# The order of the recurrence's strided views, and the row length of accumulating DMA transfers

## The chip, the cores and the metric

The kernel runs on one core of a Trainium2 chip. The metric is device time in microseconds (us) of one execution, as the median of several runs. The engines are named as in the profile: PE is TensorE (matmuls; PEld is its weight load), DVE is VectorE, ACT is ScalarE, POOL is GpSimd and SP is SyncE, which issues the loads. 16 DMA engines serve the core.

## The reference

One decoder block on 256 tokens of width 1024, in float32. An input projection gives the operands of two token mixers: a gated linear recurrence with 8 heads of 128 (HGRN2), and causal attention with 8 heads of 128, which at this length is one block. Each mixer's output is projected, the two are merged by sigmoid gates, projected again, added to the residual and normalised. A SwiGLU network with 2816 hidden channels and a second normalisation follow. The change touches the recurrence:

```python
step(state, (qc, kc, vc, lfc)):        # one chunk of 64 tokens
    G = cumsum(lfc)
    decay = exp(G[t] - G[s])  for s <= t, else 0
    scores = einsum('decay[t,s,d] qc[t,d] kc[s,d] -> scores[t,s]')
    o = scores @ vc + (qc * exp(G)) @ state
```

The result does not depend on the chunk length, so that a kernel may cut the 256 tokens in any other way.

## The kernel before, in words

**Tokens.** The 256 tokens lie in two halves of 128. The second half is mirrored (ORDER), so that the two halves count their tokens towards each other. Features are on the partitions, and the free dimension of the recurrence's tiles is (half u, head h, token t), 2 x 8 x 128 = 2048 floats; one half of a tile is 4 KB.

**The recurrence by levels** (hgrn_steps). Instead of 64-token chunks, the kernel doubles: at level l, runs of n = 2^l tokens are paired with the next run of n tokens, for l from 0 to 6, and the scores of each pair are made by one matmul per head. Qt holds the queries times the decay so far, Kt the keys times theirs, tot the decay products of the runs, SD the scores. In each level, half of the tokens are "later" and the other half "earlier"; through the mirroring the later run of a pair in half 0 lies where the earlier run lies in half 1. The two functions `earlier` and `later` (lines 414 to 418) give a view of exactly those 1024 elements of a tile:

```python
[[P, nh], [2 * n, 64 // n], [H * P + n, NT], [1, n]]     # heads, blocks, half, tokens of a run
```

Each level then has four steps. ScalarE copies the earlier elements of Kt into KL (line 444). TensorE multiplies, head by head, KL as weights with the later elements of Qt (line 449), 8 matmuls of 128 columns in plain float32, each of which the profile shows as two records. VectorE writes those scores that belong to the same block into SD, with a predicated copy per four heads, whose mask is a constant from shape_constants (line 451). VectorE multiplies the later elements of Qt and the earlier ones of Kt by the neighbour's decay (lines 458 and 459), and makes tot of the next level (line 462).

**Other work of that time.** These steps stand among the products of the input projection, with which TensorE goes on between them. side.step() in the program interleaves the two. Outside of stretches in manual_schedule, a scheduler sets the order of the instructions on each engine from its own estimates.

**Weights.** Each weight tile of 1 MB comes in by a load on SP's queue (line 223, 128 rows of 8 KB, three buffers), ScalarE rounds it to the high part wh (line 224), VectorE subtracts to get the low part wl (line 226), and TensorE uses both in three products. A load can start when VectorE has read the buffer's previous content; the high and low parts have four buffers each.

**Weight sums.** For some products (gate hg, values mv, down projection) a scheme with 7 instead of 8 block products is used, which needs sums of weight blocks. The sums are made by DMA alone, from DRAM to DRAM (sum_weights, line 235): four plain copies and four accumulating transfers for each of four groups, 16 accumulating transfers of 1 MB in all. They are issued on POOL's queue one after the other, in the order of SUMS, each behind a tiny instruction on POOL that waits for a certain weight tile (SUMS_WITH). An accumulating transfer waits for the transfers that made its operands, and the weight load of a sum (raw<-u) waits for the last of them. The row length of the accumulating ones is set by max_dma_last_dim, 2048 bytes.

Of the kernel before, what the change touches and what calls it, by code (L numbers as in the profile page):

```python
# [14 lines left out]
ALU = mybir.AluOpType  # L15
# [40 lines left out]
def shape_constants():  # L56
    c = np.zeros((P, C_END), np.float32)
    i = np.arange(P)
    c[:, C_CAUSAL:C_CAUSAL + P] = np.where(i[None, :] <= i[:, None], 0.0, NEG)
    c[:, C_CAUSAL + 2 * P:C_MASK] = np.where(i[None, :] >= i[:, None], 0.0, NEG)  # L60
    half = P // 2
    inv = np.float32(10000.0) ** (-np.arange(half, dtype=np.float32) / np.float32(half))
    ang = np.arange(T, dtype=np.float32)[:, None] * inv.astype(np.float32)[None, :]
    cos = np.cos(ang.astype(np.float64)).astype(np.float32)[ORDER].T
    sin = np.sin(ang.astype(np.float64)).astype(np.float32)[ORDER].T
    c[:, C_COS:C_COS + T] = np.concatenate([cos, cos], 0)
    c[:, C_SIN:C_SIN + T] = np.concatenate([-sin, sin], 0)
    for l in range(LEVELS):
        n = 2 ** l
        b, r = i >> (l + 1), (i >> l) & 1  # L70
        m = (b[:, None, None, None] == np.arange(64 // n)[None, :, None, None]) & \
            (r[:, None, None, None] == np.arange(2)[None, None, :, None]) & np.ones((1, 1, 1, n), bool)
        c[:, C_MASK + l * P:C_MASK + (l + 1) * P] = m.reshape(P, P)
    return np.concatenate([np.eye(P, dtype=np.float32), c], 1)

# [68 lines left out]
def hybrid_layer_kernel(ctx: ExitStack, tc, x, xT, vecs, wts, ln1_w, ln1_b, ln2_w, ln2_b, consts, out):  # L144
# [90 lines left out]
    def sum_weights(behind):  # L235


        n = len(SUMS_WITH) - len(sums)
        dst, src, add = sums.pop(0)
        tick = ticks[:, n:n + 1]  # L240
        nc.vector.tensor_copy(tick, behind)  # L241
        tc.keep_in_program_order(nc.gpsimd.tensor_tensor(mark, tick, tick, op=ALU.add))  # L242
        more = dict(accum_op=ALU.add, max_dma_last_dim=2048) if add else {}
        tc.keep_in_program_order(nc.gpsimd.dma_start(source(dst), source(src), **more))  # L244

    def fetch(ahead=LOOKAHEAD):
# [162 lines left out]
    def free_view(ap, offset, dims):  # L409
        return bass.AP(ap.tensor, ap.offset + offset, [ap.ap[0]] + dims)  # L410
# [1 line left out]


    def earlier(z, n, h0=0, nh=H):
        return free_view(z, h0 * P, [[P, nh], [2 * n, 64 // n], [H * P + n, NT], [1, n]])

    def later(z, n, h0=0, nh=H):
        return free_view(z, h0 * P + n, [[P, nh], [2 * n, 64 // n], [H * P - n, NT], [1, n]])

    def hgrn_steps():  # L420
        Qt, SD = halves(slot("Qt")), halves(slot("SD"))
        nc.vector.tensor_mul(Qt, Qg, Fg)
        flat = lambda z: z.rearrange("p u h t -> p (u h t)")
        kq, kqh, kql = flat(Qg), slot("kqh", F32R), slot("kql", F32R)
        nc.vector.tensor_mul(kq, flat(Kt), kq)
        nc.scalar.copy(kqh, kq)
        nc.vector.tensor_sub(kql, kq, r32(kqh))
        for g in range(4):
            ps = aux.tile([P, 4, P], F32, tag="aux", name=f"sd{g}")
            cs = slice(g * 512, (g + 1) * 512)  # L430
            row = ps.rearrange("p h t -> p (h t)")
            nc.tensor.matmul(row, ones, kqh[:, cs], start=True, stop=False)
            nc.tensor.matmul(row, ones, kql[:, cs], start=False, stop=True)
            nc.vector.tensor_tensor(SD[:, g // 2, 4 * (g % 2):4 * (g % 2) + 4, :], ps,
                                    ident[:, None, :].to_broadcast([P, 4, P]), op=ALU.mult)
        yield
        Tt = slot("Tt")
        tot, size = Fg, NT * H * P
        off = 0
        for l in range(LEVELS):  # L440
            n = 2 ** l
            nb = 64 // n
            KL = klp.tile([P, H, P], F32, tag="kl", name=f"kl{l}")
            nc.scalar.copy(KL.rearrange("p h (b u i) -> p h b u i", u=NT, i=n), earlier(Kt, n))
            for g in range(2):
                ps = aux.tile([P, 4, P], F32, tag="aux", name=f"sc{l}_{g}")
                for a in range(4):
                    h = 4 * g + a
                    nc.tensor.matmul(ps[:, a, :], KL[:, h, :], later(Qt, n, h, 1), start=True, stop=True)  # L449
                m = masks[:, l, :].rearrange("p (b u i) -> p b u i", u=NT, i=n)  # L450
                nc.vector.copy_predicated(later(SD, n, 4 * g, 4),
                                          m[:, None, :, :, :].to_broadcast([P, 4, nb, NT, n]),
                                          ps.rearrange("p a (b u i) -> p a b u i", u=NT, i=n))

            first = free_view(tot, 0, [[2, H * nb], [size // NT + 1, NT], [0, n]])
            second = free_view(tot, 1, [[2, H * nb], [size // NT - 1, NT], [0, n]])
            flat = lambda z: z.rearrange("p h b u i -> p (h b) u i")
            nc.vector.tensor_mul(flat(later(Qt, n)), flat(later(Qt, n)), first)
            nc.vector.tensor_mul(flat(earlier(Kt, n)), flat(earlier(Kt, n)), second)
            if l < LEVELS - 1:  # L460
                nxt = Tt[:, off:off + size // 2]
                nc.vector.tensor_mul(nxt, free_view(tot, 0, [[2, size // 2]]), free_view(tot, 1, [[2, size // 2]]))
                off += size // 2
                tot, size = nxt, size // 2
            yield
        SL = klp.tile([P, H, P], F32, tag="kl", name="SL")
        for g in range(2):
            ps = aux.tile([P, 4, P], F32, tag="aux", name=f"sc7_{g}")
            for a in range(4):
                nc.tensor.matmul(ps[:, a, :], Kt[:, 0, 4 * g + a, :], Qt[:, 1, 4 * g + a, :], start=True, stop=True)  # L470
            nc.scalar.copy(SL[:, 4 * g:4 * g + 4, :], ps)
        yield
        yah[:] = [slot("yah", F32R).rearrange("p (h t) -> p h t", h=H)]
        yal[:] = [slot("yal", F32R).rearrange("p (h t) -> p h t", h=H)]
        for g in range(2):
            for u in range(NT):
                ps = aux.tile([P, 4, P], F32, tag="aux", name=f"o{g}{u}")
                for a in range(4):
                    h = 4 * g + a
                    hd = slice(h * P, (h + 1) * P)  # L480
                    if u == 1:
                        nc.tensor.matmul(ps[:, a, :], SL[:, h, :], hv[:, 0, hd], start=True, stop=False)
                    nc.tensor.matmul(ps[:, a, :], SD[:, u, h, :], hv[:, u, hd], start=(u == 0), stop=True)
                sq = hd2.tile([P, 4, P], F32, tag="sg", name=f"sq{g}{u}")
                st = sm.tile([P, 12], F32, tag="ost", name=f"ost{g}{u}")
                for a in range(4):
                    nc.scalar.activation(sq[:, a, :], ps[:, a, :], AF.Square, accum_out=st[:, a:a + 1])
                nc.vector.tensor_scalar(st[:, 4:8], st[:, 0:4], 1.0 / P, RMS_EPS, op0=ALU.mult, op1=ALU.add)
                nc.gpsimd.tensor_tensor(st[:, 8:12], st[:, 4:8], half, op=ALU.pow)
                row = hgs[:, u, g * 512:(g + 1) * 512].rearrange("p (a d) -> p a d", a=4)  # L490
                nc.vector.tensor_mul(row, row, ps)
                for a in range(4):
                    nc.scalar.mul(row[:, a, :], row[:, a, :], st[:, 8 + a:9 + a])
            yield
            for j in range(2):
                h0 = 4 * g + 2 * j
                pt = aux.tile([P, 2, T], F32, tag="aux", name=f"ot{g}{j}")
                for a in range(2):
                    for u in range(NT):
                        hd = slice((h0 + a) * P, (h0 + a + 1) * P)  # L500
                        nc.tensor.transpose(pt[:, a, u * P:(u + 1) * P], hgs[:, u, hd], ident)
                for a in range(2):
                    h = h0 + a
                    nc.scalar.activation(yah[0][:, h, :], pt[:, a, :], AF.Copy, scale=nw[:, h:h + 1])
                    nc.vector.scalar_tensor_tensor(yal[0][:, h, :], pt[:, a, :], nw[:, h:h + 1], r32(yah[0][:, h, :]),
                                                   op0=ALU.mult, op1=ALU.subtract)
        yield
# [487 lines left out]
```

## Time and profile before

| | us |
|---|---|
| median of 3 runs | 501.06 (501.01 to 501.81) |
| the profiled execution's own time | 501.59 |
| its span | 499.5 |
| PE busy | 488.8 |
| DVE busy | 380.5 |
| ACT busy | 299.3 |
| POOL busy | 92.4 |

The span is the time from the first to the last recorded instruction of one execution; the rest of the execution's own time lies around it. A group of instructions is named by line, engine and operation, and tiles by their names in the program, without buffer numbers. A time on the chain that ended last is time that the end depended on. A row of waits reads: the waiting engine and line, what released it, the total in us, how many times, and the longest. In the table by stretch, the DMA share is the mean busy share of the 16 engines, and can be a little over 1 where two transfers overlap on an engine.

### The profile page before, as it was taken

How to read it: one execution, taken by the hardware profiler on the slowest of the kernel's cores; microseconds unless marked ns; L12 is line 12 of the kernel's file. 1: busy time of each engine (PE TensorE's matmuls, PEld its weight loads, DVE VectorE, ACT ScalarE, POOL GpSimd, SP SyncE). 2: the span in 40 equal slices, each digit the busy share in tenths (PEclk: the TensorE clock that was granted, in tenths of full speed). 3: DMA queues.
4: the chain of work that ended last, by engine and by line, in shares of the span. 5: the costliest groups of instructions: out<-in, count | busy, mean ns of one | idle time of the engine just before them, and what ended most of it. 6: DMA issues, size and time to landing. Idle time of an engine off the chain costs nothing.

```text
span 499.5 us, 7868 instructions
## 1 busy us (share of the span) xinstructions
PE 488.8 (98%) x3176; PEld 447.8 (90%) x3176; DVE 380.5 (76%) x441; ACT 299.3 (60%) x396; POOL 92.4 (18%) x97
## 2 busy tenths in 40 slices
PE   8999999999999999999999999999999999999993
PEld 8999889999999999999999988888888888898883
DVE  4678889977788588689855789566687679688856
ACT  6698655427498779697553443354665666586610
POOL 0003370320000243377400000002212011000001
PEclk9999999999999999999999999999999999999997
DMA  7989999989998997649856555249999999999802
GB/s 241 363 298 365 368 309 319 248 322 308 349 337 261 308 339 244 241 166 411 295 226 228 193 207 211 88 168 357 290 312 320 343 312 306 300 337 371 289 1 85
DMA packets 26404, 137.83 MB, mean 276 GB/s; under 512 B 2560, under 2 KB 3712, under 8 KB 14592
## 3 DMA queue, kind: packets, MB, share of 16 engines
q1 hardware_dynamic: 16560, 100.63, 53.6%
q0 software_dynamic: 9808, 36.70, 28.3%
q8 instruction: 25, 0.41, 0.3%
q14 instruction: 11, 0.09, 0.1%
HBM read 136.27 MB, written 34.60 MB: 342 GB/s over the span
## 4 chain that ended last, share of the span: by engine, by line
PE 93%; DMA 3%; DVE 1%; SPq 1%; issue 0%; ACT 0%; DVEq 0%
PE fu L846 7%; PE fg L846 7%; PE fg L847 3%; PE fu L847 3%; DMA raw<-in_wts_dram 3%; PE sc L449 3%; PE wd L929 2%; PE wd L930 2%; PE wd L931 2%; PE mk L321 2%; PE zb L321 2%; PE zb L320 2%; PE zb L319 2%; PE hq L321 2%; PE hq L320 2%; PE hq L319 2%
## 5 line engine op out<-in xcount | busy, mean ns | idle before, releaser
L226 DVE TENSOR_TENSOR wl<-raw,wh 128x2048 fp32r<-128x2048 f32 (+2 forms) x100 | 214.6, 2149 | 76.9 <-ACT wh L224 76.6
L224 ACT CAST wh<-raw 128x2048 fp32r<-128x2048 f32 (+2 forms) x100 | 179.0, 1792 | 103.0 <-DMA raw<-in_wts_dram 26.5
L846 PE MATMUL fg<-x1p,wh 128*128 128x512 f32 x144 | 50.5, 394 | 0.0
L846 PE MATMUL fu<-x1p,wh 128*128 128x512 f32 x144 | 50.4, 394 | 0.0
L242 POOL TENSOR_TENSOR mark<-ticks 128x1 f32<-128x1 f32 x32 | 24.3, 760 | 135.6 <-DVE ticks L241 135.5
L847 PE MATMUL fg<-x1p,wl 128*128 128x256 f32 x144 | 40.0, 277 | 0.0
L847 PE MATMUL fu<-x1p,wl 128*128 128x256 f32 x144 | 39.9, 277 | 0.0
L846 PEld LDWEIGHTS fu<-x1p,wh 128*128 128x128 f32 x144 | 27.0, 187 | 6.2
L846 PEld LDWEIGHTS fg<-x1p,wh 128*128 128x128 f32 x144 | 27.0, 187 | 6.1
L847 PEld LDWEIGHTS fg<-x1p,wl 128*128 128x128 f32 x144 | 27.0, 188 | 0.1
L847 PEld LDWEIGHTS fu<-x1p,wl 128*128 128x128 f32 x144 | 27.0, 188 | 0.0
L244 POOL DMA_DIRECT2D u<-u x8 | 8.2, 1020 | 65.3 <-DMA u<-u 22.6
L319 PE MATMUL hf<-xTh,wh 128*128 128x256 f32 x64 | 19.1, 298 | 0.9 <-ACT wh L224 0.9
L321 PE MATMUL hf<-xTh,wl 128*128 128x256 f32 x64 | 19.0, 298 | 0.6 <-DVE wl L226 0.6
L244 POOL DMA_DIRECT2D u<-in_wts_dram x24 | 17.5, 732 | 10.0 <-DMA u<-in_wts_dram 8.5
L319 PE MATMUL za<-yah,wh 128*128 128x256 f32 x64 | 18.9, 295 | 0.0
L320 PE MATMUL hf<-xTl,wh 128*128 128x256 f32 x64 | 18.8, 294 | 0.0
L319 PE MATMUL mq<-xTh,wh 128*128 128x256 f32 x64 | 18.5, 289 | 0.0
L319 PE MATMUL mk<-xTh,wh 128*128 128x256 f32 x64 | 18.4, 287 | 0.0
L321 PE MATMUL mk<-xTh,wl 128*128 128x256 f32 x64 | 18.3, 286 | 0.0
L319 PE MATMUL gb<-xTh,wh 128*128 128x256 f32 x64 | 18.3, 286 | 0.0
L321 PE MATMUL ga<-xTh,wl 128*128 128x256 f32 x64 | 18.3, 285 | 0.0
(310 smaller groups left out, 1463.9 us busy)
## 6 DMA issues: line engine op xcount, KB each, us to landing
raw<-in_wts_dram SPq DMA_DIRECT2D x74, 1024.0 KB, 6.7
raw<-u SPq DMA_DIRECT2D x16, 1024.0 KB, 8.0
u<-in_wts_dram POOLq DMA_DIRECT2D x8, 1024.0 KB, 20.2
u<-u POOLq DMA_DIRECT2D x8, 1024.0 KB, 18.9
raw<-in_wts_dram SPq DMA_DIRECT2D x8, 256.0 KB, 4.8
xTr<-in_xT_dram SPq DMA_DIRECT2D x8, 128.0 KB, 4.8
raw<-in_wts_dram SPq DMA_DIRECT2D x2, 512.0 KB, 6.5
xr<-in_x_dram POOLq DMA_DIRECT2D x1, 1024.0 KB, 8.6
```

Of the source, the lines that this page charges most:

```text
L224: nc.scalar.copy(h[:, ks, :], raw[:, ks, :])
L226: eng.tensor_sub(l[:, ks, :], raw[:, ks, :], r32(h[:, ks, :]))
L242: tc.keep_in_program_order(nc.gpsimd.tensor_tensor(mark, tick, tick, op=ALU.add))
L244: tc.keep_in_program_order(nc.gpsimd.dma_start(source(dst), source(src), **more))
L319: nc.tensor.matmul(ps, wh[:, k, wcol], ah[:, kk, :], start=(kk == 0), stop=False)
L320: nc.tensor.matmul(ps, wh[:, k, wcol], al[:, kk, :], start=False, stop=False)
L321: nc.tensor.matmul(ps, wl[:, k, wcol], ah[:, kk, :], start=False, stop=(kk == KC - 1))
L449: nc.tensor.matmul(ps[:, a, :], KL[:, h, :], later(Qt, n, h, 1), start=True, stop=True)
L846: nc.tensor.matmul(ps, wh[:, k, wcol], x1p.both(k), start=(k == 0), stop=False)
L847: nc.tensor.matmul(ps[:, 0, :], wl[:, k, wcol], x1p[0, k, slice(0, T)], start=False, stop=(k == KC - 1))
L929: nc.tensor.matmul(ps, lh[:, k, :], wh[:, k, ns], start=n < 5 and i + k == 0, stop=False, **go)
L930: nc.tensor.matmul(ps, lh[:, k, :], wl[:, k, ns], start=False, stop=False, **go)
```

## The change

Three things change together, and the constants of the masks with them.

1. The views `earlier` and `later` go through the half first, then heads, blocks and the tokens of a run. They name the same elements in another order. The copy into KL, the moving operand of the score matmuls, the predicated copies and the columns of the masks follow that order.
2. The two products of a level on all 1024 elements become four, one per half, each on 512.
3. The accumulating transfers have rows of up to 8192 bytes.

```diff
@@ shape_constants
-        m = (b[:, None, None, None] == np.arange(64 // n)[None, :, None, None]) & \
-            (r[:, None, None, None] == np.arange(2)[None, None, :, None]) & np.ones((1, 1, 1, n), bool)
+        m = (b[:, None, None, None] == np.arange(64 // n)[None, None, :, None]) & \
+            (r[:, None, None, None] == np.arange(2)[None, :, None, None]) & np.ones((1, 1, 1, n), bool)
@@ sum_weights
-        more = dict(accum_op=ALU.add, max_dma_last_dim=2048) if add else {}
+        more = dict(accum_op=ALU.add, max_dma_last_dim=8192) if add else {}
@@
     def earlier(z, n, h0=0, nh=H):
-        return free_view(z, h0 * P, [[P, nh], [2 * n, 64 // n], [H * P + n, NT], [1, n]])
+        return free_view(z, h0 * P, [[H * P + n, NT], [P, nh], [2 * n, 64 // n], [1, n]])
 
     def later(z, n, h0=0, nh=H):
-        return free_view(z, h0 * P + n, [[P, nh], [2 * n, 64 // n], [H * P - n, NT], [1, n]])
+        return free_view(z, h0 * P + n, [[H * P - n, NT], [P, nh], [2 * n, 64 // n], [1, n]])
@@ hgrn_steps
-            nc.scalar.copy(KL.rearrange("p h (b u i) -> p h b u i", u=NT, i=n), earlier(Kt, n))
+            nc.scalar.copy(KL.rearrange("p h (b u i) -> p u h b i", u=NT, i=n), earlier(Kt, n))
...
-                m = masks[:, l, :].rearrange("p (b u i) -> p b u i", u=NT, i=n)
+                m = masks[:, l, :].rearrange("p (u b i) -> p u b i", u=NT, i=n)
                 nc.vector.copy_predicated(later(SD, n, 4 * g, 4),
-                                          m[:, None, :, :, :].to_broadcast([P, 4, nb, NT, n]),
-                                          ps.rearrange("p a (b u i) -> p a b u i", u=NT, i=n))
-
-            first = free_view(tot, 0, [[2, H * nb], [size // NT + 1, NT], [0, n]])
-            second = free_view(tot, 1, [[2, H * nb], [size // NT - 1, NT], [0, n]])
-            flat = lambda z: z.rearrange("p h b u i -> p (h b) u i")
-            nc.vector.tensor_mul(flat(later(Qt, n)), flat(later(Qt, n)), first)
-            nc.vector.tensor_mul(flat(earlier(Kt, n)), flat(earlier(Kt, n)), second)
+                                          m[:, :, None, :, :].to_broadcast([P, NT, 4, nb, n]),
+                                          ps.rearrange("p a (u b i) -> p u a b i", u=NT, i=n))
+
+            side = lambda z, off, u: free_view(z, off + u * H * P, [[2 * n, H * nb], [1, n]])
+            whole = lambda off: free_view(tot, off, [[2, H * nb], [0, n]])
+            for u in range(NT):
+                q, k = side(Qt, n - u * n, u), side(Kt, u * n, u)
+                nc.vector.tensor_mul(q, q, whole(u * (size // NT + 1)))
+                nc.vector.tensor_mul(k, k, whole(1 + u * (size // NT - 1)))
```

The order of the instructions on the engines stays nearly the same. On DVE, around the end of level 0 and the start of level 1 (sc_0_805 and sc_1_811 are the scores of level 0, wl the low part of a weight tile), there stands before:

```order
L451 COPY_PREDICATED SD<-cst,sc_0_805 128x256x2
L458 TENSOR_TENSOR Qt<-Qt,Fg 128x512x2
L241 COPY ticks<-wl_857 128x1
L462 TENSOR_TENSOR Tt<-Tt 128x128
L451 COPY_PREDICATED SD<-cst,sc_1_811 128x256x2
L226 TENSOR_TENSOR wl_895<-raw_893,wh_894 128x2048
L462 TENSOR_TENSOR Tt<-Tt 128x64
L459 TENSOR_TENSOR Kt<-Kt,Tt 128x256x2x2
```

And at the same place on DVE after the change:

```order
L451 COPY_PREDICATED SD<-cst,sc_0_805 128x2x256
L459 TENSOR_TENSOR Qt<-Qt,Fg 128x512 x2
L241 COPY ticks<-wl_859 128x1
L463 TENSOR_TENSOR Tt<-Tt 128x128
L451 COPY_PREDICATED SD<-cst,sc_1_811 128x2x256
L226 TENSOR_TENSOR wl_897<-raw_895,wh_896 128x2048
L463 TENSOR_TENSOR Tt<-Tt 128x64
L460 TENSOR_TENSOR Kt<-Kt,Tt 128x256x2 x2
```

Nothing has changed places; the products stand twice, and the views have the half ahead of the rest. Lines from 459 on have moved down by one.

On PE, where the score matmuls of level 0 stand among the gate product gb of the input projection, there stands before:

```order
L319 MATMUL gb_903<-xTh,wh_768 128x256
L449 MATMUL sc_0_805<-Qt,kl_803 128x128 x4
L449 MATMUL sc_1_811<-Qt,kl_803 128x128 x4
L320 MATMUL gb_903<-xTl,wh_768 128x256
L321 MATMUL gb_903<-xTh,wl_769 128x256
```

And at the same place on PE after the change:

```order
L319 MATMUL gb_905<-xTh,wh_768 128x256
L320 MATMUL gb_905<-xTl,wh_768 128x256
L449 MATMUL sc_0_805<-Qt,kl_803 128x128 x4
L449 MATMUL sc_1_811<-Qt,kl_803 128x128 x4
L321 MATMUL gb_905<-xTh,wl_769 128x256
```

The eight score matmuls of level 0 have moved behind one more matmul of gb. The matmuls of sd (line 433) move by one in the same way; the other rows of PE stand as they stood.

On POOL, the sums of the first group (u_3072: the gate hg) have before:

```order
L244 DMA u_3072_0_388<-in_wts_dram 512x512
L242 TENSOR_TENSOR mark<-ticks 128x1
L244 DMA u_3072_0_453<-in_wts_dram 512x512
L242 TENSOR_TENSOR mark<-ticks 128x1
L244 DMA u_3072_0_741<-in_wts_dram 16x16384
L242 TENSOR_TENSOR mark<-ticks 128x1
L244 DMA u_3072_0_516<-u_3072_0_388 512x512
```

And on POOL after the change:

```order
L244 DMA u_3072_0_388<-in_wts_dram 128x2048
L242 TENSOR_TENSOR mark<-ticks 128x1
L244 DMA u_3072_0_453<-in_wts_dram 128x2048
L242 TENSOR_TENSOR mark<-ticks 128x1
L244 DMA u_3072_0_741<-in_wts_dram 16x16384
L242 TENSOR_TENSOR mark<-ticks 128x1
L244 DMA u_3072_0_516<-u_3072_0_388 128x2048
```

The order is the same, and so are the plain copies (16 rows); the accumulating transfers have 128 rows of 2048 floats in place of 512 rows of 512.

## The prediction

> **What bounds the kernel now.** I read the page's first part, then what TensorE waited for, then a table by stretch, then the chain that ended last.
>
> ```profile
> span 499.5 us, 7868 instructions
> PE 488.8 (98%) x3176; PEld 447.8 (90%) x3176; DVE 380.5 (76%) x441; ACT 299.3 (60%) x396; POOL 92.4 (18%) x97
> ```
>
> What TensorE waited for, whole span (all of the answer):
>
> ```profile
> PE warm L366 <- DVE half L367: 1.1, 1, 1.1
> PE hf L319 <- ACT wh L224: 0.9, 1, 0.9
> PE hf L321 <- DVE wl L226: 0.6, 1, 0.6
> ```
>
> By stretch (TensorE, weight loads, VectorE, ScalarE, GpSimd busy, then granted clock, DMA share, GB/s):
>
> ```profile
> 27.00:76.00 49.00, 49.00 (x325) 45.27 (x324) 40.48 (x36) 36.28 (x39) 18.60 (x15) 1.00 0.97 338
> 76.00:91.00 15.00, 15.00 (x113) 14.65 (x112) 15.00 (x17) 7.48 (x7) 0.81 (x2) 1.00 0.81 233
> 91.00:160.00 69.00, 69.00 (x497) 65.09 (x497) 55.83 (x50) 43.52 (x43) 9.72 (x17) 1.00 1.00 316
> ...
> 330.00:427.00 97.00, 97.00 (x556) 84.66 (x555) 69.64 (x94) 58.47 (x80) 15.44 (x24) 1.00 1.00 310
> ```
>
> TensorE waits 2.6 us in all, every bit of it in the warm-up and the hf matmuls at the start, at full clock, and is busy for all of each stretch from 27 us on. So time is gained only by making matmuls shorter, and lost by anything that makes them wait. The second thing to see is the DMA share: 1.00 from 91 to 160 us and from 330 to 427 us, the two places where the accumulating transfers run. The transfer engines have nothing to spare there. Vector and Scalar time is not the bound: 55.8 and 43.5 of 69 us.
>
> **The score matmuls.** The changed views are read by TensorE only in the score matmuls of line 449. The chain gives one row per level, 16 records each (two per matmul):
>
> ```profile
> 78.48 2.67 PE sc L449 x16
> 86.77 1.92 PE sc L449 x16
> 99.85 1.79 PE sc L449 x16
> ```
>
> Level 0 takes 2.67/16 = 167 ns a record, level 1 120 ns, level 2 112 ns, and the later levels repeat 1.79. The levels differ only in the run length n of the view, 1, 2, 4 elements, after which it jumps to the other half of the tile, 4 KB away. After the change it stays in one half and skips n elements instead: level 0 reads every second element of one row of 128. I have no row of TensorE reading at that stride. Upper bound: it keeps 167 ns, since the runs are still one element long (gain 0, rival two). Lower bound: the contiguous rate, 112 ns, gain 16 x 55 = 0.88 us. Nearest row: level 1, which like the new level 0 uses two elements of each 16 bytes, 120 ns, gain 0.75 us. Level 1 itself can go from 120 to 112, gain 0 to 0.13 us. Together 0.75 to 1.01 us; I take 0.9, all of it on the path since TensorE waits for nothing here.
>
> [...]
>
> **The Vector and Scalar work.** From VectorE's timeline:
>
> ```profile
> 62.87 2.24 DVE L459 TENSOR_TENSOR Kt<-Kt,Fg 128x1024 f32<-128x1024 f32 x1
> ...
> 77.28 0.68 DVE L462 TENSOR_TENSOR Tt<-Tt 128x512 f32<-128x512 f32 x1
> ...
> 80.41 2.50 DVE L451 COPY_PREDICATED SD<-cst,sc 128x512 f32<-128x512 uint32 x1
> 82.50 2.50 DVE L458 TENSOR_TENSOR Qt<-Qt,Fg 128x1024 f32<-128x1024 f32 x1
> ...
> 89.69 1.23 DVE L459 TENSOR_TENSOR Kt<-Kt,Tt 128x1024 f32<-128x1024 f32 x1
> ...
> 90.98 1.33 DVE L451 COPY_PREDICATED SD<-cst,sc 128x512 f32<-128x512 uint32 x1
> ...
> 108.32 0.73 DVE L451 COPY_PREDICATED SD<-cst,sc 128x512 f32<-128x512 uint32 x1 [1.38 <-PE sc L449]
> ```
>
> The products: each product of 1024 elements becomes two of 512. The 512-element product at 77.28 reads both operands at a stride of two and takes 0.68, so a pair is 1.36. At level 0 that replaces 2.24 and 2.50: 2.0 us less. At levels 1 to 6 it replaces 1.23 or so, 12 times: 12 x 0.13 = 1.6 us more. The predicated copies of level 0 (2.50, twice) go to between 0.73 and 1.33 (level 1): 2.3 to 3.5 us less. The Scalar copy into kl at level 0 goes from its longest (1590 ns) to its median:
>
> ```profile
> L444 ACT COPY kl<-Kt x7: 1031/1051/1590, 32.5 to 141.0; 128x1024 f32<-128x1024 f32 x7
> ```
>
> Net, Vector is relieved of 2.7 to 3.9 us and Scalar of 0.5. Before 91 us this is hidden behind TensorE's own work; it buys slack and no time. The 0.13 us per product that come after 91 us delay the weight subtraction (L226) queued behind them on Vector; the nearest slack on Vector is 0.9 us (below; where a tile has only 0.06 us, Vector had idled 1.64 us before it), so they are covered too. TensorE's order changes at two points by one matmul, which costs nothing: the same instructions run back to back.
>
> **The accumulating transfers.** 16 of them, 1 MB each, go from 512 rows of 2 KB to 128 rows of 8 KB. TensorE does not wait for them, but the weight loads share the engines with them. Four stretches of the DMA queues: accumulates alone (95 to 99 us), both (159 to 165), weight loads alone (181 to 185), and 2 KB rows of the output (493 to 497):
>
> ```profile
> DMA packets 395, 0.87 MB, mean 217 GB/s; under 512 B 2, under 2 KB 2, under 8 KB 394
> ```
> ```profile
> q1 hardware_dynamic: 210, 1.59, 66.4%
> q0 software_dynamic: 212, 0.43, 38.9%
> ```
> ```profile
> DMA packets 207, 1.56 MB, mean 391 GB/s; under 512 B 16, under 2 KB 16, under 8 KB 16
> q1 hardware_dynamic: 207, 1.56, 94.5%
> ```
> ```profile
> DMA packets 239, 0.46 MB, mean 116 GB/s; under 512 B 16, under 2 KB 16, under 8 KB 238
> q1 hardware_dynamic: 238, 0.45, 30.2%
> ```
>
> On 16 engines, 4 us hold 64 engine-us. Alone, a 2 KB accumulated row takes 64/393 = 163 ns and an 8 KB weight row 64/191 = 335 ns. Side by side (q1 the loads, q0 the accumulates) they go row for row, 210 to 212. That is what the change turns round. An 8 KB accumulated row is not in the trace. Upper bound: four 2 KB rows, 652 ns. Lower bound: one plain 8 KB row, 335 ns. I take the upper one less what long rows save plain transfers: 2 KB rows occupy an engine for 0.302 x 64/222 = 87 ns, four of them 348, against 0.945 x 64/191 = 317 for one of 8 KB, 9% less. So about 595 ns.
>
> A weight load is 8 rows per engine. Beside an accumulate it now takes 8 x (335 + 163) = 4.0 us and will take 8 x (335 + 595) = 7.4 us, 3.4 us more (1.4 to 3.9 by the bounds). The accumulate itself takes 32 x 498 = 15.9 us now and 7.4 then, and its own work falls from 32 x 163 = 5.2 to 8 x 595 = 4.8 us. So loads are hit harder, but for half as long, and over an accumulate and its aftermath the loads lose nothing. What covers the 3.4 us is the distance between a weight tile's subtraction and the matmul that uses it. It varies. Vector:
>
> ```profile
> 103.45 2.30 DVE L226 TENSOR_TENSOR wl<-raw,wh 128x2048 fp32r<-128x2048 f32 x1
> ...
> 140.60 2.29 DVE L226 TENSOR_TENSOR wl<-raw,wh 128x2048 fp32r<-128x2048 f32 x1 [0.50 <-ACT wh L224]
> ...
> 170.30 2.29 DVE L226 TENSOR_TENSOR wl<-raw,wh 128x2048 fp32r<-128x2048 f32 x1 [1.64 <-ACT wh L224]
> ```
>
> and the matmuls that first use these three tiles:
>
> ```profile
> 119.72 0.23 PE hg L298
> ```
> ```profile
> 143.80 0.40 PE L298 MATMUL hg<-wl,xSh 128*128 128x512 f32 x1
> ...
> 172.65 0.39 PE L321 MATMUL mk<-xTh,wl 128*128 128x256 f32 x1
> ```
>
> Slack is 119.72 - 105.75 = 14 us, then 143.80 - 142.89 = 0.9 us, then 172.65 - 172.59 = 0.06 us: it is used up exactly where the four accumulates of the value weights run. GpSimd issues them at:
>
> ```profile
> 105.99 1.05 POOL L244 DMA_DIRECT2D u<-in_wts_dram  x1 [5.14 <-DMA u<-in_wts_dram]
> ...
> 110.69 1.03 POOL L244 DMA_DIRECT2D u<-in_wts_dram  x1 [3.40 <-DMA u<-in_wts_dram]
> ...
> 126.99 1.02 POOL L244 DMA_DIRECT2D u<-u  x1 [4.74 <-DMA u<-in_wts_dram]
> ...
> 152.26 1.01 POOL L244 DMA_DIRECT2D u<-u  x1 [20.43 <-issue]
> ```
>
> The last sits behind the one before for 20 us. When accumulates land 8 us sooner, that issue moves to about 135 to 140 us, and the loads for the tiles used at 160 to 173 us meet free engines. I therefore expect the contention to move forward, towards the larger slack, and TensorE to go on without a wait. The margin is thin.
>
> **The sum.** The profiled execution took 501.59 us for its span of 499.5. Less 0.9: 500.7. The median of the three runs, 501.06, lies 0.5 below the profiled one, so 501.06 - 0.9 = **500.2 us**. About 0.2% (1.0 us) is what a measurement of this kernel can tell from no change (its runs spread over 0.8 us), and the forecast lies just inside it.
>
> **Rival one: the loads come late (slower).** At 140 to 143 us the slack is 0.9 us, and a load that spends its whole length beside an accumulate arrives up to 3.9 us later if an 8 KB row costs the full 652 ns. If the accumulate issued at 126.99 still meets the loads of the tiles used from 143 us on, TensorE stands 3.9 - 0.9 = 3.0 us once; loads behind it in the queue are late by the same amount, not by more. Total 501.06 - 0.9 + 3.0 = 503.2 us; a second, partial stall in the down projection, behind its own last four accumulates, could bring 504. It decides from the point where rows cost nearly four times 163 ns, so that nothing is saved. For it: the DMA share of 1.00 and the row-for-row sharing. Against it: the saving of 9%, and the earlier accumulates. Chance 0.26.
>
> [...]
>
> **Rival two: the matmuls stay as they are.** If single elements cost TensorE 167 ns wherever the next one lies, the time stays at 501.06 and only off-path Vector time goes. Against it: the doubled stride costs the product at 77.28 nothing on Vector. Chance 0.08.
>
> **The numbers.** Forecast (no wait, 0.75 to 1.01 us gained): 0.66. With the scatter of a median of few runs around 0.9, half of that is beyond 1.0 us: 0.33 faster, 0.33 same. Rival one 0.26: 0.24 slower, 0.02 same. Rival two 0.08: 0.06 same, 0.02 slower. In all faster 0.33, same 0.41, slower 0.26. The range reaches from the full 1.01 us and the scatter (499.6) to rival one (503.2); what lies beyond is rival one with its second stall. The likeliest case alone is 499.6 to 500.6.
>
> **What would show it.** Level 0's 16 records in about 1.8 to 1.9 us, level 1 at 1.8 to 1.9; predicated copies at level 0 below 1.4; pairs of products near 0.68 each; 128 rows per accumulate at about 595 ns alone; TensorE still without a wait after 27 us; the last value accumulate issued before 145 us. The prediction is wrong if TensorE's list of waits gains rows on wh or wl at 120 to 175 or 440 to 475 us, or if level 0 stays above 2.5 us.

## The result and the profile after

The changed kernel takes 508.79 us in the median of 5 runs (506.74 to 510.5), the kernel before 501.06 beside it. The ratio is 1.0148, with a 95% interval of 1.0118 to 1.0179: 7.4 us slower (7.7 between the two medians). The forecast was 500.2 us, with a range up to 503.2. Of all executions below two were slow, one of 984 us (8 KB rows for the down projection only) and one of 812.5 us (high part first): the ratios leave them out, the medians don't, and without them these two would be 503.5 and 506.5 us.

The profiled execution took 509.1 us, its span is 507.3. What TensorE waited for in the changed kernel (left out are the two rows of the start, 1.1 us each):

```profile
PE wd L931 <- DVE wl L226: 1.9, 1, 1.9
PE hg L298 <- DVE wl L226: 1.8, 1, 1.8
...
PE hg L297 <- ACT wh L224: 0.7, 1, 0.7
PE sc L449 <- ACT kl L444: 0.4, 1, 0.4
```

All four are new: TensorE waits for weights in the gate product hg (0.7 and 1.8 us) and in the down projection wd (1.9), and for a copy into kl (0.4).

By stretch, changed kernel, the columns as before (TensorE, weight loads, VectorE, ScalarE, GpSimd busy, granted clock, DMA share, GB/s):

```profile
76.00:91.00 15.00, 14.60 (x117) 14.09 (x116) 13.02 (x19) 10.57 (x10) 2.04 (x5) 1.00 1.03 306
91.00:160.00 69.00, 66.42 (x471) 62.10 (x471) 53.20 (x58) 40.58 (x41) 7.63 (x13) 0.98 0.92 303
...
427.00:482.00 55.00, 53.06 (x268) 45.54 (x267) 50.38 (x46) 39.31 (x38) 1.12 (x2) 0.97 0.85 313
```

TensorE is idle for 0.40 + 2.58 + 1.94 = 4.9 us, where it was idle for nothing. Two columns more have changed: the granted clock falls below 1.00 in the two stretches with a long wait, and the DMA share from 91 to 160 us falls from 1.00 to 0.92. The transfer engines now stand idle for a part of the very stretch in which TensorE waits for weights.

The first wait on TensorE's timeline (start, us, instruction, and in brackets the idle time before it and what ended it):

```profile
133.73 0.49 PE L297 MATMUL hg<-wh,xTh 128*128 128x512 f32 x1 [0.75 <-ACT wh L224]
136.06 0.50 PE L298 MATMUL hg<-wl,xTh 128*128 128x512 f32 x1 [1.83 <-DVE wl L226]
...
136.87 0.63 PE L298 MATMUL hg<-wl,xTh 128*128 128x512 f32 x1
137.30 0.63 PE L299 MATMUL hg<-wh,xTl 128*128 128x512 f32 x1
```

Behind the wait the same instruction takes 0.63 us for 0.39, and one starts 0.43 us after another, not 0.23. The stretch behind this wait, and the one behind the wait in wd, show why:

```profile
136.80:140.20 3.40, 3.40 (x9) 2.69 (x9) 3.39 (x3) 0.00 (x0) 0.81 (x1) 0.50 0.82 306
451.00:454.30 3.30, 3.30 (x15) 3.30 (x16) 3.27 (x4) 3.30 (x4) 0.00 (x0) 0.50 0.72 236
```

For about 3.4 us behind each of the two long waits TensorE is granted half its clock (0.50), and so loses 1.7 us each time. That closes the account: 4.9 us idle and 2 x 1.7 = 3.4 us at half clock make 8.3; less the 0.95 that the score matmuls gained (below), 7.4. The sum goes by the one execution that was profiled.

Where the first wait comes from, on the chain that ended last of the changed kernel:

```profile
112.87 18.88 DMA raw<-in_wts_dram
131.78 1.92 ACT wh L224
133.72 2.30 DVE wl L226
136.06 0.50 PE hg L298
```

One weight load takes 18.9 us from its issue; for over half of that time another load, issued before it, is still coming in (it is rounded at 124.46, see below). The two DMA queues show what it met (q1 the loads, q0 the sums' transfers; packets, MB, share of 16 engines). The same 24 us, 107 to 131, before:

```profile
DMA packets 1690, 7.30 MB, mean 304 GB/s; under 512 B 118, under 2 KB 118, under 8 KB 1075
...
q1 hardware_dynamic: 688, 4.98, 54.6%
q0 software_dynamic: 1000, 2.29, 47.6%
```

And after:

```profile
DMA packets 863, 7.22 MB, mean 301 GB/s; under 512 B 96, under 2 KB 96, under 8 KB 96
...
q0 software_dynamic: 429, 4.04, 69.9%
q1 hardware_dynamic: 432, 3.15, 32.6%
```

The engines move about as much as before, 7.2 MB. But the loads get 3.15 MB of it instead of 4.98, and the sums 4.04 instead of 2.29.

### The profile page after: what moved, and what is told of

The parts are those of the page before. It is cut to its first block, busy times and chain, and to the rows that moved or that the text cites. A ratio compares the mean times of both kernels' runs of the same rounds, so it can differ in the third digit from the quotient of the medians.

```text
span 507.3 us, 7882 instructions
## 1 busy us (share of the span) xinstructions
PE 492.1 (97%) x3176; PEld 449.9 (89%) x3176; DVE 376.1 (74%) x455; ACT 297.6 (59%) x396; POOL 78.9 (16%) x97
## 4 chain that ended last, share of the span: by engine, by line
PE 75%; DMA 13%; DVE 4%; ACT 4%; issue 1%; SPq 1%; DVEq 0%; ACTq 0%
DMA raw<-in_wts_dram 12%; PE fu L847 7%; PE fg L847 7%; PE fg L848 3%; PE fu L848 3%; DVE wl L226 3%; ACT wh L224 3%; PE wd L931 2%; PE wd L930 2%; PE wd L932 2%; PE sc L449 2%; PE zb L321 2%; PE zb L320 2%; PE zb L319 2%; PE mq L321 2%; PE mq L320 2%
## 5 line engine op out<-in xcount | busy, mean ns | idle before, releaser
L242 POOL TENSOR_TENSOR mark<-ticks 128x1 f32<-128x1 f32 x32 | 12.6, 394 | 177.6 <-DVE ticks L241 173.6
L319 PE MATMUL za<-yah,wh 128*128 128x256 f32 x64 | 18.9, 295 | 0.0
L321 PE MATMUL za<-yah,wl 128*128 128x256 f32 x64 | 18.3, 285 | 0.0
L320 PE MATMUL za<-yal,wh 128*128 128x256 f32 x64 | 18.2, 285 | 0.0
L321 PE MATMUL mq<-xTh,wl 128*128 128x256 f32 x64 | 18.2, 284 | 0.0
```

The lines of the kernel that those rows point to most:

```text
L319: nc.tensor.matmul(ps, wh[:, k, wcol], ah[:, kk, :], start=(kk == 0), stop=False)
L320: nc.tensor.matmul(ps, wh[:, k, wcol], al[:, kk, :], start=False, stop=False)
L321: nc.tensor.matmul(ps, wl[:, k, wcol], ah[:, kk, :], start=False, stop=(kk == KC - 1))
```

## The experiments

Two theories at the start. **A**: the long rows cost everything. Beside an accumulate, a load gets a third of the engines (32.6% above); TensorE stalls twice, and the clock falls behind each stall. **B**: the views and the split products cause the stalls or share in them, by more instructions ahead of the weight subtractions on VectorE.

### The views without the long rows, and the long rows without the views

The changed kernel with

```
-        more = dict(accum_op=ALU.add, max_dma_last_dim=8192) if add else {}
+        more = dict(accum_op=ALU.add, max_dma_last_dim=2048) if add else {}
```

> The changed kernel with the accumulating transfers back in rows of 2 KB; views and products stay split by half. Theory A (the long rows cost everything: the loads get a third of the engines where they had two thirds, which stalls TensorE twice, and the clock falls to half for 3.4 us behind each stall): 500.1 us, 0.9 below the kernel before (ratio 0.998), no wait of TensorE on wl or wh after 27 us, granted clock 1.00 from 91 to 160 us, level 0 of the scores at 1.79. Theory B (the split products put more instructions ahead of the weight subtractions on VectorE and cause the stalls, or part of them): 504 us or more, with waits on wl in the gate product hg.

Measured: 500.08 us, ratio 0.9968 (0.9956 to 0.9981). Its waits of TensorE (all), and its score matmuls of levels 0, 1 and 2 on the chain:

```profile
PE warm L366 <- DVE half L367: 1.1, 1, 1.1
PE hf L319 <- ACT wh L224: 1.0, 1, 1.0
```
```profile
78.38 1.82 PE sc L449 x16
85.71 1.82 PE sc L449 x16
98.68 1.79 PE sc L449 x16
```

No wait is left after the start. Level 0 went from 2.67 to 1.82 us and level 1 from 1.92 to 1.82: 0.95 us gained. The ratio says 1.6 us (0.95 to 2.2); the runs of before spread over 2 us on that chip, and what the rest of it is stays open.

The opposite, the kernel before with that one line at 8192:

> The kernel before with nothing changed but the rows of the accumulating transfers, 8 KB for 2 KB. Theory A: the whole loss and no gain, 501.1 + 7.4 + 0.9 = 509.4 us (508.4 to 510.4, ratio 1.015 to 1.019), both stalls and both half-clock stretches there, level 0 of the scores at 2.67. Theory B: 501 to 503 us.

Measured: 509.17 us, ratio 1.0154 (1.0129 to 1.0178). Its waits on weights, and the one in hg on the timeline:

```profile
PE wd L930 <- DVE wl L226: 2.1, 2, 1.9
PE hg L298 <- DVE wl L226: 1.5, 1, 1.5
```
```profile
135.51 0.50 PE L298 MATMUL hg<-wl,xTh 128*128 128x512 f32 x1 [1.52 <-DVE wl L226]
135.85 0.40 PE L299 MATMUL hg<-wh,xTl 128*128 128x512 f32 x1
```

Theory B falls with these two runs. The whole loss comes with the rows, in the same places and with no view changed, and the views with the split products alone gain. One part of the expectation missed: behind the 1.5 us in hg the clock did not fall (1.00 from 133.5 to 140 us).

### Rows of 4 KB

> The changed kernel with accumulating rows of 4 KB. By theory A a row should cost about 178 + (628 - 178)/3 = 328 ns alone, and a weight load beside an accumulate 8 x (335 + 328) = 5.3 us where it was 4.0 with 2 KB and 7.7 with 8 KB. The least slack of before was 0.9 us, so that a stall of some tenths of a us is possible: 500.1 to 503 us, 501 likeliest. Theory B: within 1 us of the changed kernel, 508 us.

Measured: 501.8 us, ratio 1.0000 (0.9988 to 1.0012). Its waits on weights after the start, and its queues from 107 to 113 us:

```profile
PE ga L319 <- ACT wh L224: 0.7, 1, 0.7
PE mv L297 <- ACT wh L224: 0.3, 1, 0.3
```
```profile
q1 hardware_dynamic: 147, 1.07, 50.3%
q0 software_dynamic: 142, 0.56, 47.1%
```

And the changed kernel with 8 KB, 125 to 131 us:

```profile
q0 software_dynamic: 111, 0.90, 72.0%
q1 hardware_dynamic: 107, 0.76, 31.8%
```

With 16 engines, 6 us are 96 engine-us. A 4 KB row takes 0.471 x 96/142 = 318 ns, an 8 KB row 0.720 x 96/111 = 623 ns. Again the queues go nearly row for row (142 to 147 packets with 4 KB, 111 to 107 with 8 KB). A load is 1.05 MB in the units of these views. Beside an accumulate with 8 KB rows it so takes 6 x 1.05/0.76 = 8.3 us, with 4 KB rows 6 x 1.05/1.07 = 5.9, and with 2 KB rows (1.59 MB in 6 us, in the prediction's rows) 4.0. Added up from the rows it is 8 x (335 + 623) = 7.7, 5.2 and 4.0 us. What TensorE needs can be read from the prediction's rows: the tiles subtracted at 103.45 and at 170.30 are 13 apart, 5.1 us a tile. A load of 4.0 us keeps pace, one of 5.2 to 5.9 just about or not quite, and one of 7.7 to 8.3 falls some 3 us further behind each time. That order is the order of the three times: 500.1, 501.8, 508.8. But the step from 500.1 to 501.8 is small and in part has another source: in the profiled execution with 4 KB rows TensorE also waits 3.0 us in hf at the start, before the first sum is issued, against 1.0 us with 2 KB.

### Which accumulates make which wait

The changed kernel with 8 KB rows in one part of the sums and 2 KB in the other (n counts the 32 transfers; the gate and the values are the first 16). For the down projection only, and then for the gate and the values only:

```
-        more = dict(accum_op=ALU.add, max_dma_last_dim=8192) if add else {}
+        more = dict(accum_op=ALU.add, max_dma_last_dim=8192 if n >= 16 else 2048) if add else {}
...
+        more = dict(accum_op=ALU.add, max_dma_last_dim=8192 if n < 16 else 2048) if add else {}
```

> The changed kernel with 8 KB rows in the sums of the down projection only, 2 KB in those of the gate and the values. Theory A with each stall made by the accumulates of its own stage: the wait in hg and its half-clock stretch go (about 3.0 + 1.7 us), the one in the down projection stays (about 2.2 + 1.7 us less the 0.9 gained): 504 us (503 to 505). Rival: the loads fall behind once, in the first stage, and stay late to the end: then the second stall goes too, 500.1 us. Theory B: as the changed kernel, 508 us.

> The changed kernel with 8 KB rows in the sums of the gate and the values only, 2 KB in those of the down projection: the complement of the run with 8 KB there only (504.0 us). If the two losses are separate and add up to the whole 508.8: 508.8 - 504.0 + 500.1 = 504.9 us (504 to 506), with a wait in the gate product hg and none in the down projection. If the first loss also feeds the second: above 506.5 us, with a wait on wl in the down projection.

Measured: 503.97 us (ratio 1.0042, 1.0025 to 1.0059) for the down projection, 504.46 (1.0052, 1.0028 to 1.0077) for the gate and the values. Waits on weights after the start, of the first and of the second:

```profile
PE wd L931 <- DVE wl L226: 2.2, 2, 1.9
```
```profile
PE hg L298 <- DVE wl L226: 1.8, 1, 1.8
PE hg L297 <- ACT wh L224: 0.3, 1, 0.3
```

The two losses are separate and add up: in ratios 1.0042 + 1.0052 - 0.9968 = 1.0126, against 1.0148 (1.0118 to 1.0179) for the whole. The rival, one delay carried through to the end, falls.

The second wait does not come beside an accumulate: the last one is issued at 408.12 us and lands 14.6 us later, and TensorE waits from 449 us on. ScalarE's roundings of the tiles show what lies between. At 384.90 us the changed kernel is 4.06 us later than the kernel before, which the first loss has left. The next five tiles each wait for their load (392.22, 400.34, 407.75, 415.21 and 422.90 us), and with the last of them it is 14.4 us later. After that it catches up, but at the tile rounded at 446.69 us 10.4 are left, more than that tile had in hand. There the rounding no longer waits for its load; on the chain it stands behind other work of ScalarE and VectorE.

### Time between the accumulates

Is one 8 KB accumulate too much, or the row of them? In the changed kernel GpSimd issues three of the values' accumulates at 100.15, 108.42 and 120.14 us, and the page gives 14 us from issue to landing (these three land at 115.1, 122.5 and 133.0): one is still under way when the next is issued, and so from 100.15 to 133.0 us there always is one. The changed kernel with

```
-SUMS_WITH = (6, 7, 8, 9, 10, 11, 12, 14, 13, 15, 16, 17, 18, 19, 20, 22,
+SUMS_WITH = (6, 7, 8, 9, 10, 11, 12, 14, 13, 15, 16, 19, 21, 22, 24, 26,
```

> The changed kernel, 8 KB rows included, with the four accumulating transfers of the values tied to the weight tiles 19, 21, 24 and 26 instead of 17, 18, 20 and 22 (the plain copy between them to 22), so that two tiles or so lie between one and the next. Theory A1 (a debt that adds up: beside an accumulate a load gets a third of the engines, which is less than TensorE consumes; between accumulates it wins back 4.35 - 2.7 = 1.6 us a tile): no wait in the gate product hg at 133 us, the second wait in the down projection stays: 504 us (503.3 to 505.5). Theory A2 (one 8 KB accumulate by itself makes the loads beside it too late): the waits only move on to 140 to 170 us, where before had 0.9 us of slack and less, and the time stays at 507 to 510 us.

Measured: 504.86 us, ratio 1.0087 (1.0054 to 1.012). Issues of the first two of them on GpSimd, and what TensorE waited for weights behind the start:

```profile
116.71 0.84 POOL L244 DMA_DIRECT2D u<-in_wts_dram  x1
...
129.81 0.82 POOL L244 DMA_DIRECT2D u<-in_wts_dram  x1
```
```profile
PE wd L931 <- DVE wl L226: 1.7, 1, 1.7
```

The rows are 8 KB still and the same transfers run, yet hg waits for nothing. That profile is of the fastest of the six executions (503.54 us); two others took 508.2 and 509.5 us, and what they waited for isn't recorded. So it is a debt that adds up (A1): ScalarE's rounding of the tiles, which here starts when a load has landed, shows it. In the changed kernel three in turn come at

```profile
115.11 1.90 ACT L224 CAST wh<-raw 128x2048 fp32r<-128x2048 f32 x1 [3.03 <-DMA raw<-in_wts_dram]
...
124.46 1.91 ACT L224 CAST wh<-raw 128x2048 fp32r<-128x2048 f32 x1 [6.37 <-DMA raw<-u]
...
131.78 1.91 ACT L224 CAST wh<-raw 128x2048 fp32r<-128x2048 f32 x1 [3.98 <-DMA raw<-in_wts_dram]
```

so 9.4 and 7.3 us apart (8.3 on average, as worked out above), where TensorE uses a tile in 5.1 on average. Before, the same three came at 117.48, 121.19 and 127.07: the changed kernel is 2.4 us ahead with the first and 4.7 late with the third, the one that TensorE waits for. With the accumulates spread, that third one comes at 122.21.

### A wait for wh in place of one for wl

In the changed kernel, the products of a block with the high part go first, in block_product and, in the same way, in quad_product:

```
         for k in range(KQ // 2):
             nc.tensor.matmul(ps, lh[:, k, :], wh[:, k, :], start=first and k == 0, stop=False, **go)
-            nc.tensor.matmul(ps, lh[:, k, :], wl[:, k, :], start=False, stop=False, **go)
-            nc.tensor.matmul(ps, ll[:, k, :], wh[:, k, :], start=False, stop=k == KQ // 2 - 1, **go)
+            nc.tensor.matmul(ps, ll[:, k, :], wh[:, k, :], start=False, stop=False, **go)
+        for k in range(KQ // 2):
+            nc.tensor.matmul(ps, lh[:, k, :], wl[:, k, :], start=False, stop=k == KQ // 2 - 1, **go)
```

> The changed kernel, 8 KB rows included, but in the products of the gate, the values and the down projection the eight matmuls with the high part wh of a block go ahead of the four with the low part wl. TensorE then needs wl 8 matmuls after wh and not 1: 8 x 0.23 = 1.84 us later with 512 columns, 8 x 0.12 = 0.96 us with 256. Theory A (the price is the wait for a late wl, and the half clock follows from the length of that wait): 1.6 us of the first wait and 0.8 of the second go, and the half-clock stretch behind the first with its 1.7 us: 508.8 - 1.6 - 0.8 - 1.7 = 504.7 us (503.0 to 506.5). If wh, not wl, were what TensorE really waits for, nothing goes: 508 us.

Measured: 506.77 us, ratio 1.0103 (1.0083 to 1.0123): a gain of 2 us, less than expected. The same kernel ran once more, for its profile:

> The kernel with the wh products ahead of the wl products once more, for its profile: the 506.8 us measured lie 2.1 above what was expected. Theory A: the first wait is down to some tenths of a us and without a half-clock stretch; the rest sits in the down projection, where 256 columns give only 0.96 us of cover. Rival: the half clock comes behind shorter waits too, so that both stretches are still there.

Measured: 506.5 us, ratio 1.0099 (1.0078 to 1.0119). By stretch, and the longest wait of TensorE:

```profile
76.00:91.00 15.00, 13.83 (x108) 13.23 (x107) 12.20 (x17) 9.34 (x9) 1.55 (x3) 1.00 1.00 306
91.00:160.00 69.00, 67.36 (x486) 63.09 (x486) 53.72 (x61) 39.72 (x40) 8.11 (x14) 1.00 0.95 312
...
427.00:482.00 55.00, 52.59 (x269) 44.42 (x268) 50.40 (x45) 40.39 (x39) 1.12 (x2) 1.00 0.85 309
```
```profile
PE ga L320 <- ACT wh L224: 1.6, 1, 1.6
```

TensorE is idle for 1.17 + 1.64 + 2.41 = 5.2 us, no less than the 4.9 of the changed kernel. My expectation was wrong there: a later need of wl doesn't make the load come sooner. In hg, TensorE pays the lateness at the next tile's wh (1.6 us, at 138.89). The rest is spread: 1.1 for wl and 0.4 for wh in the down projection, 0.9 there for a result that ScalarE still had to move, and 1.2 for a copy into kl before 91 us. Why these other waits grew was not followed up. What did go is the half clock: 1.00 in all stretches from 27 to 482 us, with 1.6 us as the longest wait in them. Both the expectation and its rival were half right.

### The half clock by itself

The kernel with 2 KB rows, in which VectorE subtracts the last weight tile several times over (the result is the same), so that TensorE waits near the end with no transfer in the way:

```
-            eng.tensor_sub(l[:, ks, :], raw[:, ks, :], r32(h[:, ks, :]))
+            for _ in range(3 if i == len(loads) - 1 else 1):
+                eng.tensor_sub(l[:, ks, :], raw[:, ks, :], r32(h[:, ks, :]))
```

> The changed kernel with 2 KB rows (500.1 us), in which VectorE subtracts the last weight tile of the down projection three times over, with the same result. That tile has about 2.8 us of slack, and each subtraction takes 2.2: TensorE then stands still for about 1.6 us, once, with no transfer in the way. If a wait costs its own length and no more: 501.7 us. If one of 1.6 us already brings the clock to half for 3.4 us: 503.4 us.

> As the run before, with the last tile subtracted four times: TensorE stands for about 3.8 us. If a wait costs its own length: 503.9 us. If it brings the clock to half for 3.4 us behind it: 505.6 us, and the records behind the wait are spaced at twice the time (0.43 us for 512 columns instead of 0.23).

Measured: 500.86 and 501.48 us (ratios 0.999 and 1.0005). Nothing was tested: the tile had more slack than I had read, and neither profile has a wait there (with four, single executions took up to 505.2 us, and these have no profile). So with five and six:

> The changed kernel with 2 KB rows (500.1 us), the last weight tile of the down projection subtracted five times over. With four the subtraction ended at 482.18 and TensorE's first matmul with that tile ran at 482.23: the slack was just used up. A fifth, 2.3 us, should make TensorE stand for 2.3 to 2.5 us with no transfer in the way. If a wait costs its own length and no more: 502.5 us. If it brings the clock to half for 3.4 us: 504.2 us.

> The same with six subtractions: TensorE stands for about 4.7 us. If a wait costs its own length: 504.8 us. With the half clock behind it: 506.5 us, and records of 512 columns spaced at 0.43 us instead of 0.23 for 3.4 us.

Measured: 506.68 us (503.88 to 508.72) and 508.26 (506.87 to 510.41). TensorE's timeline with five, and two stretches of it:

```profile
481.68 0.39 PE L710 MATMUL wd<-wh,ah 128*128 128x512 f32 x1
486.08 0.80 PE L711 MATMUL wd<-wl,ah 128*128 128x512 f32 x1 [4.01 <-DVE wl L227]
486.67 0.63 PE L712 MATMUL wd<-wh,al 128*128 128x512 f32 x1
```
```profile
478.00:481.60 3.60, 3.60 (x17) 2.98 (x17) 3.53 (x3) 0.00 (x0) 0.00 (x0) 1.00 0.00 0
486.20:491.20 5.00, 5.00 (x12) 3.98 (x13) 1.83 (x3) 0.00 (x0) 0.00 (x0) 0.50 0.01 3
```

The wait came out at 4.0 us and not 2.4, because the run of subtractions started later in this execution (474.43 us, against 472.91 with four), so both numbers expected are too low. But it decides: with no DMA traffic at all (share 0.00 and 0.01) the clock is at 0.50 for 5 us behind the wait, and 500.1 + 4.0 + 2.5 = 506.6 us is the time that was measured. With six, the wait is 6.1 us, the half clock lasts 5.6 us behind it, and 500.1 + 6.1 + 2.8 = 509.0 us stands against 509.49 in the profiled execution. So in these two runs the half clock came behind a wait of TensorE's own, with no transfer in the way.

## Why the prediction was wrong

**Score matmuls: right.** 0.75 to 1.01 us forecast, 0.9 taken, 0.95 measured in the kernel with 2 KB rows. Both levels now run at 1.82/16 = 114 ns a record. Level 0 came out nearer to the lower bound (112 ns) than to the nearest row (120 ns). Level 1 got faster too (120 to 114 ns), with runs as long as before; what has changed in its view is that it no longer jumps to the other half, 4 KB away, after each run.

**Vector and Scalar work: right.** Changed kernel, predicated copies by group (minimum, median, maximum in ns), and a pair of products:

```profile
L451 DVE COPY_PREDICATED SD<-cst,sc x14: 710/730/1332, 82.7 to 152.8; 128x512 f32<-128x512 uint32 x14
```
```profile
88.77 1.29 DVE L460 TENSOR_TENSOR Kt<-Kt,Tt 128x512 f32<-128x512 f32 x2
```

The longest copy fell from 2495 to 1332 ns, and a pair of products takes 1.29 where 1.36 was forecast. The kernel with 2 KB rows, in which TensorE waits for nothing after the start, shows that the added instructions hold nothing up. In the changed kernel one pair (109.36 us, 1.28 us) does stand on the chain, ahead of the late load; with the old views and 8 KB rows the single product stands there with 1.21 us.

**Row and load: nearly right.** 623 ns for an 8 KB accumulated row (595 forecast, at most 652), 7.7 us by the rows or 8.3 by the bytes for a load beside it (7.4 forecast, 7.9 by its upper bound).

**"Over an accumulate and its aftermath the loads lose nothing": the step that failed.** It set the loads' loss beside one accumulate, "for half as long", against the quiet behind it. Neither half of that came. An accumulate was to last 7.4 us in place of 15.9; the three issued at 100.15, 108.42 and 120.14 us took 14.9, 14.1 and 12.9 us to land, 33 us in all with two plain copies of the same queue among them, where the same three had taken 46 us before. And there is no quiet between them: the next accumulate has been issued when one lands, and with the faster ones the next starts sooner (the third at 120.14 us, before at 126.99). From 107 to 131 us the loads beside them move 3.15 MB, not 4.98. The quiet comes when the third has landed: from 134 to 138 us the DMA share is 0.43, but TensorE is already waiting. Nor can it be used for loads further ahead, since three buffers hold them back: the next load is issued at 136.03 us, when the late tile's subtraction ends and frees a buffer. The number that decides it was at hand, 7.4 us a load, and the pace of the tiles (5.1 us) could be read from the trace; the prediction never set one against the other. Nor did it look at the tile that TensorE then waited for: before, it was subtracted by 131.29 us and needed at 133.54, 2.2 us of slack against a delay of 4.7. That the contention "moves forward, towards the larger slack" was right (the last of the values' accumulates was issued at 136.83 us, as forecast before 145), but the 14 us of slack were taken for enough without a sum.

**Rival one: right in kind, too small in size.** It had late loads, a wait in hg (at 143 us; it came two tiles earlier, at 134 to 136) and a second stall in the down projection. Its price was one wait of 3.0 us; hg waited 2.6 and wd another 1.9. What it lacked is the half clock, 2 x 1.7 us, and its "late by the same amount, not by more" doesn't hold: each load beside an accumulate adds some 3 us. So 504 us at most became 508.8. The row-for-row sharing that it leaned on shows with 8 KB rows too: 111 packets of the sums against 107 of the loads from 125 to 131 us, where a packet is a row (0.90 MB in the 111).

**Rival two: wrong**, the matmuls did get shorter.

The experiments also leave a kernel that beats both: the changed views and products with rows of 2 KB, 500.08 us, ratio 0.9968 (0.9956 to 0.9981) to before.

## What to carry to other kernels

In three stretches of 6 us with an accumulate beside the loads, the two DMA queues moved nearly as many rows as each other, with rows of 2, 4 and 8 KB in the sums (212 to 210, 142 to 147, 111 to 107). So the length of the sums' rows worked as a priority: with 8 KB for 2 KB the loads moved 3.15 MB in 24 us and not 4.98. Work out how long a load takes beside the other queue's transfer, and set it against the time in which the compute engine uses one load's data; if it is longer, each load adds to a debt, and the slack divided by that debt says how many it takes until the engine stops. And price a stall of TensorE with what comes behind it, not only with its own length: here waits of 1.8 and 1.9 us cost 1.7 us more each.

## What the runs showed of the hardware

**Waits of 1.8 to 6.1 us were followed by half the clock.** Waits of 1.5 (hg in the kernel before with 8 KB rows), 1.6 (ga, high part first) and 1.7 us (wd, accumulates spread) left the granted clock at 1.00; waits of 1.8, 1.9, 4.0 and 6.1 us were followed by 0.50, for 3.3 to 3.4 us behind the shorter ones, 5 us behind the one of 4.0 and 5.6 us behind the one of 6.1.

In the changed kernel the granted clock falls at 136.83 us, 0.8 us behind the end of the wait in hg, and at 450.86, 0.1 us before the end of the one in wd; it is back 3.41 us later each time. What parts the waits of 1.7 us from those of 1.8, and whether the length alone does, is not shown: no run varied the length or the place of a wait between the two.

**An accumulated row cost nearly by its length.** 163 ns alone or 176 beside loads (0.389 x 96/212) with 2 KB, 318 with 4 KB, 623 with 8 KB, both beside loads: long rows saved an accumulate only 4 to 12% here, where a plain row of 8 KB took 335 ns.
